# Dividing the softmax of an attention core after its value product, with the reciprocals spread over the rows by an identity product

## The chip, the core and the metric

The kernel is one program on one core of a Trainium2 chip. The metric is device time in microseconds of one execution. The engines named below are PE (TensorE, matmuls), PEld (its weight loads), DVE (VectorE), ACT (ScalarE), POOL (GpSimd) and SP (it issues the DMAs). Each of them takes its instructions strictly in the order in which they stand in its queue, and waits on semaphores for the others.

## The reference

Four layers over 256 context tokens and 256 latent tokens of width 1024. Layers 0 and 3 mix tokens by windowed grouped-query attention with a sink logit for each head, layer 1 by latent attention (MLA), layer 2 by a linear recurrence; a gated MLP with a short convolution follows each. What the change concerns is the softmax and the product behind it:

```python
def attend(q, k, v, mask=None, sink=None):
    s = jnp.einsum("bqhgd,bkhd->bhgqk", q, k, preferred_element_type=jnp.float32) * (q.shape[-1] ** -0.5)
    ...
    m = jnp.max(s, axis=-1)
    ...
    p = jnp.exp(s - m[..., None])
    denom = jnp.sum(p, axis=-1)
    if sink is not None:
        denom = denom + jnp.exp(sk - m)
    o = jnp.einsum("bhgqk,bkhd->bqhgd", p, v.astype(jnp.float32))
    o = o / jnp.transpose(denom, (0, 3, 1, 2))[..., None]
```

## The kernel before

Everything lives feature by token: the stream `X` is eight tiles of 128 features by 512 tokens. Weights come in units of 128 x 1024, one DMA each, and are split into a high and a low part (`whi` by ACT, `wlo` by POOL); a projection is then three matmuls for each tile (lines 231 to 233). Layers 0, 1 and 2 work on all 512 tokens and layer 3 on the latent ones alone.

Attention is cut into *cores*, a function `core` in `swa` (layers 0 and 3) and one in `mla` (layer 1). One core is a block of 128 queries for two heads `z` = 0, 1. There are 32 cores in layer 0 (16 on context blocks with 256 keys, 16 on latent blocks with 512), 32 in layer 1 (16 and 16) and 16 in layer 3 (latent alone): 80 in all. A core does, in this order:

- the scores of both heads into a PSUM bank `mm` (L678, L679; in MLA L920), queries on the partitions;
- the row maximum. In a latent core of `swa` one DVE instruction adds the mask, scales and takes the maximum (L705), and another negates it (L708). Elsewhere it is a reduction and a few small ones;
- the exponentials `P` by ACT with the row sums `den` (L709, L698; in MLA L930), and in `swa` the sink's part of the sum (L711 to L713);
- the reciprocals `rd` of the sums, 128 x 2 (L714, L931);
- the division, on `P`, while the queries are still on the partitions and the reciprocal is a scalar of each partition: in `swa` head 0 by DVE (L719) and head 1 by ACT (L717), in MLA both by DVE (L933);
- the transposes of `P` on PE (L727, L941), copied out of the bank `tp` to `pt` by ACT, in `swa` every second one by DVE (L249, L251);
- the value product into the bank `mo` (L733, L947): head 0 fills partitions 0 to 63 and head 1 partitions 64 to 127, 128 columns (queries) wide;
- `put`, which splits the result into `o` high (ACT, L265) and `o` low (DVE, L266).

Pools set how far cores can overlap: two banks each of `mm`, `tp`, `mo` and `fl`, six tiles `P`, two `pt`. In layer 0 the products that make the modulation vectors (`mod0_steps`, L346) keep one of the two `mo` banks for as long as they last: 26 steps, of which 3 are taken in the projection ahead of the cores and one by each core after, so 23 of the 32 cores share the other bank. Between cores stand projections: those of the next queries or keys in bank `fl`, and the output projection of the first half of the heads.

The order on each engine is set when the program is built, by a scheduler that interleaves the cores with the projections; at run time each engine goes through its list and waits where an input is missing.

Of the kernel before, what the change touches and what calls it, by code (L numbers as in the profile page):

```python
# [14 lines left out]
AF = mybir.ActivationFunctionType  # L15
# [96 lines left out]
def hybrid_kernel(ctx: ExitStack, tc: tile.TileContext, xT, cc, ccT, W, modwa, modwb, modw, colv, rowv, tabs, band, out, depth=DEPTH, dbg=None):  # L112
# [43 lines left out]
    def mo_ps():  # L156
        return ps_mo.tile([128, T], F32, tag="mo", name="mo")
# [84 lines left out]
    def sel(arrs, *idx):  # L242
        return tuple(a[idx] for a in arrs)
# [20 lines left out]
    def split(hi, lo, src):  # L264
        nc.scalar.activation(hi, src, AF.Copy)  # L265
        nc.vector.tensor_tensor(lo, src, f32(hi), op=ALU.subtract)  # L266

    def rsqrt(v, n, steps=3):
        i = small(n, "rs_i", I32)
# [289 lines left out]
    def swa(l, i, q0, nm, nxt, first=None):  # L559
# [87 lines left out]
        def q_post(p, b, ps):  # L647
            if rqs[p] is None:
                rqs[p] = const.tile([128, 32], F32, tag=f"rqs{p}", name="rqs")
            if (p, b // 2) not in qt:  # L650
                qt[p, b // 2] = big("q").rearrange("p (b j) n -> p b j n", b=2)
            qb = qt[p, b // 2][:, b % 2]
            sq = tmp("sq")
            nc.scalar.activation(sq, ps, AF.Square)
            ss = small(8, "ssq")
            nc.vector.tensor_reduce(ss, sq.rearrange("p (h d) -> p h d", d=64), axis=AX.X, op=ALU.add)
            qr = tmp("qr")
            rotate(qr, ps, b, 8, gq, cgq, sgq)
            for z in range(2):
                hl = tmp("qhl")  # L660
                h4 = hl.rearrange("p (h s d) -> p h s d", h=4, s=2)
                q4 = qr[:, z * 256:(z + 1) * 256].rearrange("p (h d) -> p h d", h=4)
                nc.scalar.activation(h4[:, :, 0].bitcast(F32R), q4, AF.Copy)
                nc.vector.tensor_tensor(h4[:, :, 1], q4, h4[:, :, 0], op=ALU.subtract)
                pq = tp_ps()
                for j in range(4):
                    nc.tensor.transpose(pq[:, j * 128:(j + 1) * 128], hl[:, j * 128:(j + 1) * 128], ident)
                if z == 0:
                    nc.scalar.activation(qb[:, z], pq, AF.Copy)
                else:  # L670
                    nc.vector.tensor_copy(qb[:, z], pq)
            rq = mean_rsqrt(ss, 8, 64)
            nc.vector.tensor_scalar(rqs[p][:, b * 8:(b + 1) * 8], rq, 0.125, None, op0=ALU.mult)

        def scores(ps, p, b, j, g, nk):
            h = 2 * j + g
# [4 lines left out]
        def core(p, b, j):  # L681
# [19 lines left out]
            else:  # L701
                for z in range(2):
                    ps, pt = mm_ps(), probs()
                    scores(ps, p, b, j, z, nk)
                    nc.vector.tensor_tensor_reduce(  # L705
                        out=pt, in0=ps, in1=mask[:, b - 2], op0=ALU.add, op1=ALU.max,
                        scale=rq2[:, z:z + 1], scalar=sk[:, z:z + 1], accum_out=mx[:, z:z + 1])
                    nc.vector.tensor_scalar(ngm[:, z:z + 1], mx[:, z:z + 1], -1.0, None, op0=ALU.mult)  # L708
                    nc.scalar.activation(pt, pt, AF.Exp, bias=ngm[:, z:z + 1], accum_out=den[:, z:z + 1])  # L709
                    P.append(pt)  # L710
            nc.vector.tensor_tensor(es, sk, ngm, op=ALU.add)  # L711
            nc.scalar.activation(es, es, AF.Exp)
            nc.vector.tensor_tensor(den, den, es, op=ALU.add)  # L713
            nc.vector.reciprocal(rd, den)  # L714
            for z in range(2):
                if z:
                    nc.scalar.activation(P[z], P[z], AF.Copy, scale=rd[:, z:z + 1])  # L717
                else:
                    nc.vector.tensor_scalar(P[z], P[z], rd[:, z:z + 1], None, op0=ALU.mult)  # L719
            po = mo_ps()[:, :128]  # L720
            pt = pt_p.tile([128, 2, T], F32, tag="pt", name="pt")
            for kp in range(nk // 256):
                pp = tp_ps()
# [5 lines left out]
                for kk in range(2):  # L729
                    kb = 2 * kp + kk  # L730
                    for z in range(2):
                        r = slice(64 * z, 64 * z + 64)
                        nc.tensor.matmul(po[r], v[0][:, kb, p * 128 + 64 * z:p * 128 + 64 * z + 64],  # L733
                                         pt[:, kp, (kk * 2 + z) * 128:(kk * 2 + z + 1) * 128], start=kb == 0, stop=kb == nk // 128 - 1)
            put(sel(o[p], slice(None), j, slice(b * 128, (b + 1) * 128)), po)

        ps = {b: mm_ps() if z < 2 else fl_ps() for z, b in enumerate(range(q0, 4))}
        proj(1, ps, hook=lambda q, done: steps(mods, MQ[q]))
# [27 lines left out]
    def mla(l, nm, nxt):  # L766
# [138 lines left out]
        def core(hg, hp, b):  # L905
# [23 lines left out]
            for z in range(2):  # L929
                nc.scalar.activation(P[z], S[z], AF.Exp, bias=ngm[:, z:z + 1], scale=rq2[:, z:z + 1], accum_out=den[:, z:z + 1])  # L930
            nc.vector.reciprocal(rd, den)  # L931
            for z in range(2):
                nc.vector.tensor_scalar(P[z], P[z], rd[:, z:z + 1], None, op0=ALU.mult)  # L933
            po = mo_ps()[:, :128]
            pt = pt_p.tile([128, 2, T], F32, tag="pt", name="pt")
            for kp in range(nk // 256):
                pp = tp_ps()
# [5 lines left out]
                for kk in range(2):  # L943
                    kb = 2 * kp + kk
                    for z in range(2):
                        c = hp * 128 + 64 * z
                        nc.tensor.matmul(po[64 * z:64 * z + 64], d["v"][:, kb, c:c + 64], pt[:, kp, (kk * 2 + z) * 128:(kk * 2 + z + 1) * 128],  # L947
                                         start=kb == 0, stop=kb == nk // 128 - 1)
            put(sel(o[hg // 2], slice(None), (2 * hg + hp) % 4, bc), po)

        group(0)
        ss = small(16, "ssk")
# [416 lines left out]
```

## Time and profile before

| | us |
|---|---|
| median of 3 runs | 2230.91 (2227.56 to 2233.28) |
| the profiled execution | 2228.39 |
| its span, first to last instruction | 2226.6 |
| PE busy | 2113.2 (95%) |
| PEld busy | 1760.3 (79%) |
| DVE busy | 1563.7 (70%) |
| ACT busy | 1032.2 (46%) |
| POOL busy | 1044.8 (47%) |
| mean granted clock of PE | 0.987 |

The profiled execution took 1.8 us more than its span. The shares are means over stages that differ: in the MLPs PE is busy all the time, in the attention stages (the cores run from 100 to 264 us, 720 to 895 us and 1930 to 2012 us) it waits now and then, and DVE and ACT are fuller. PE counts as busy until a matmul has drained, so that overlapping matmuls make it look fuller than it is; the time of one row is no price of one matmul in a stream of them.

### The profile page before, as it was taken

How to read it: one execution, taken by the hardware profiler on the slowest of the kernel's cores; microseconds unless marked ns; L12 is line 12 of the kernel's file. 1: busy time of each engine (PE TensorE's matmuls, PEld its weight loads, DVE VectorE, ACT ScalarE, POOL GpSimd, SP SyncE). 2: the span in 40 equal slices, each digit the busy share in tenths (PEclk: the TensorE clock that was granted, in tenths of full speed). 3: DMA queues.
4: the chain of work that ended last, by engine and by line, in shares of the span. 5: the costliest groups of instructions: out<-in, count | busy, mean ns of one | idle time of the engine just before them, and what ended most of it. 6: DMA issues, size and time to landing. Idle time of an engine off the chain costs nothing.

```text
span 2226.6 us, 32884 instructions
## 1 busy us (share of the span) xinstructions
PE 2113.2 (95%) x12084; PEld 1760.3 (79%) x12084; DVE 1563.7 (70%) x3342; ACT 1032.2 (46%) x1850; POOL 1044.8 (47%) x760
## 2 busy tenths in 40 slices
PE   6989999999999999999999998899999999898999
PEld 4666788888888666878888886688888888678999
DVE  4677779777786887687888689847864457785333
ACT  4466653222346775532233367534333224675544
POOL 3331255544544113445455446764544444526887
PEclk9999999999999999999999999999999999999999
DMA  7534136554532011255555422234655552313665
GB/s 299 199 123 133 39 123 189 171 177 157 179 116 68 21 29 57 60 189 178 175 184 182 149 67 67 89 94 136 194 183 167 168 161 85 104 39 107 188 182 160
DMA packets 83888, 300.14 MB, mean 135 GB/s; under 512 B 11152, under 2 KB 12816, under 8 KB 81296
## 3 DMA queue, kind: packets, MB, share of 16 engines
q1 hardware_dynamic: 83728, 298.05, 42.2%
q8 instruction: 95, 1.56, 0.3%
q14 instruction: 65, 0.53, 0.1%
HBM read 296.97 MB, written 1.05 MB: 134 GB/s over the span
## 4 chain that ended last, share of the span: by engine, by line
PE 78%; DVE 12%; ACT 3%; DMA 3%; issue 2%; POOL 2%; SPq 0%; ACTq 0%; DVEq 0%; POOLq 0%
PE fl L232 9%; PE fl L233 9%; PE fl L231 9%; PE mm L233 7%; PE mm L232 7%; PE mm L231 7%; PE mo L231 4%; PE mo L232 4%; PE mo L233 4%; PE tp L231 3%; PE tp L232 3%; PE tp L233 3%; PE mo L733 2%; POOL wlo L222 2%; PE mm L920 2%
## 5 line engine op out<-in xcount | busy, mean ns | idle before, releaser
L222 POOL TENSOR_TENSOR wlo<-raw,whi 128x256 fp32r<-128x256 f32 (+3 forms) x709 | 1010.1, 1446 | 1113.3 <-ACT whi L218 1075.1
L218 ACT ACTIVATE whi<-raw 128x1024 fp32r<-128x1024 f32 (+3 forms) x367 | 382.5, 1043 | 489.1 <-PE mm L232 170.4
L380 DVE SCALAR_TENSOR_TENSOR junk<-mw,cbc 128x1024 bf16<-128x1024 f32 x256 | 457.3, 1786 | 26.4 <-DMA mw<-in_modw_dram 15.8
L233 PE MATMUL fl<-h_hi,wlo 128*128 128x512 f32 (+1 forms) x816 | 293.4, 360 | 4.9 <-POOL wlo L222 4.9
L231 PE MATMUL fl<-h_hi,whi 128*128 128x512 f32 (+1 forms) x816 | 293.2, 359 | 1.5 <-DVE xc L1039 1.3
L232 PE MATMUL fl<-h_lo,whi 128*128 128x512 f32 (+1 forms) x816 | 293.2, 359 | 0.0
L232 PE MATMUL mm<-h_lo,whi 128*128 128x512 f32 (+1 forms) x784 | 274.1, 351 | 2.5 <-DVE h_lo L448 1.5
L231 PE MATMUL mm<-h_hi,whi 128*128 128x512 f32 (+1 forms) x784 | 273.9, 351 | 1.2 <-ACT h_hi L442 1.1
L233 PE MATMUL mm<-h_hi,wlo 128*128 128x512 f32 (+1 forms) x784 | 273.5, 349 | 0.0
L1145 DVE SCALAR_TENSOR_TENSOR conv<-mm,colt,conv 128x510 f32<-128x510 f32 (+1 forms) x88 | 59.8, 679 | 190.1 <-ACT conv L1143 190.0
L1149 ACT ACTIVATE conv<-conv 128x512 f32<-128x512 f32 (+1 forms) x88 | 51.0, 579 | 289.3 <-DVE conv L1147 289.3
L233 PEld LDWEIGHTS fl<-h_hi,wlo 128*128 128x128 f32 x816 | 155.0, 190 | 28.6 <-POOL wlo L222 6.1
L231 PEld LDWEIGHTS fl<-h_hi,whi 128*128 128x128 f32 x816 | 155.3, 190 | 24.3 <-ACT P L1058 1.7
L232 PEld LDWEIGHTS fl<-h_lo,whi 128*128 128x128 f32 x816 | 155.0, 190 | 22.1
L232 PEld LDWEIGHTS mm<-h_lo,whi 128*128 128x128 f32 x784 | 149.4, 191 | 23.5 <-POOL h_lo L446 2.5
L231 PEld LDWEIGHTS mm<-h_hi,whi 128*128 128x128 f32 x784 | 149.4, 191 | 20.8 <-ACT h_hi L442 2.1
L233 PEld LDWEIGHTS mm<-h_hi,wlo 128*128 128x128 f32 x784 | 149.5, 191 | 18.6
L454 DVE SCALAR_TENSOR_TENSOR x<-mo,modc,x 128x256 f32<-128x256 f32 x197 | 88.3, 476 | 87.4 <-PE mo L233 87.1
L231 PE MATMUL mo<-g_hi,whi 128*128 128x512 f32 (+1 forms) x388 | 134.3, 346 | 0.6 <-DVE x L454 0.6
L232 PE MATMUL mo<-g_lo,whi 128*128 128x512 f32 (+1 forms) x388 | 134.4, 346 | 0.0
L233 PE MATMUL mo<-g_hi,wlo 128*128 128x512 f32 (+1 forms) x388 | 134.3, 346 | 0.0
L231 PE MATMUL tp<-g_hi,whi 128*128 128x512 f32 (+1 forms) x352 | 124.0, 352 | 1.5 <-DVE x L454 1.5
(331 smaller groups left out, 4427.9 us busy)
## 6 DMA issues: line engine op xcount, KB each, us to landing
raw<-in_W_dram SPq DMA_DIRECT2D x352, 512.0 KB, 3.6
mw<-in_modw_dram SPq DMA_DIRECT2D x144, 512.0 KB, 4.2
mw<-in_modwa_dram SPq DMA_DIRECT2D x8, 1024.0 KB, 14.8
mw<-in_modwb_dram SPq DMA_DIRECT2D x16, 512.0 KB, 4.9
mw<-in_modwb_dram SPq DMA_DIRECT2D x8, 1024.0 KB, 9.1
cbc<-in_cc_dram SPq DMA_DIRECT2D x3, 1024.0 KB, 6.1
raw<-in_W_dram SPq DMA_DIRECT2D x8, 384.0 KB, 3.0
x<-in_xT_dram SPq DMA_DIRECT2D x8, 256.0 KB, 4.7
```

Of the source, the lines that this page charges most:

```text
L218: nc.scalar.activation(hi, raw, AF.Copy)
L222: nc.gpsimd.tensor_tensor(lo[:, cs], raw[:, cs], f32(hi[:, cs]), op=ALU.subtract)
L231: nc.tensor.matmul(ps, ah, bh, start=start and i == 0, stop=False, **kw)
L232: nc.tensor.matmul(ps, ah, bl, start=False, stop=False, **kw)
L233: op = nc.tensor.matmul(ps, al, bh, start=False, stop=stop and i == n - 1, **kw)
L380: nc.vector.scalar_tensor_tensor(junk, raw, 1.0, cbc[:, s], op0=ALU.mult, op1=ALU.mult, accum_out=modc[l][:, s, m:m + 1])
L454: nc.vector.scalar_tensor_tensor(X[m][:, half], ps[:, half], modc[l][:, s, part + m:part + m + 1], X[m][:, half], op0=ALU.mult, op1=ALU.add)
L733: nc.tensor.matmul(po[r], v[0][:, kb, p * 128 + 64 * z:p * 128 + 64 * z + 64], pt[:, kp, (kk * 2 + z) * 128:(kk * 2 + z + 1) * 128], start ...
L920: nc.tensor.matmul(ps[:, c], d["q"][:96, 2 * hp + z, bc], d["k"][:96, 2 * hp + z, :nk], start=True, stop=True)
L1145: op = nc.vector.scalar_tensor_tensor(y3[:, :, 1:], g3[:, :, :255], cw[:, l, 0, f:f + 1], y3[:, :, 1:], op0=ALU.mult, op1=ALU.add)
L1149: nc.scalar.activation(y[:, t0:], y[:, t0:], AF.Silu)
```

## The change

The division moves from `P` to the value product. A new function `divide` gets the whole `mo` bank: columns 0 to 127 hold the value product as before, columns 128 to 255 a second product, made for each head from the reciprocals, broadcast along 64 columns as the stationary operand, and the identity as the moving one. It puts the reciprocal of query n into column n of all 64 rows of a head. ACT copies these 128 x 128 numbers to SBUF (into `P[0]`, which the transposes no longer need), DVE multiplies the value product by them in place, and `put` follows as before. Both scalings of `P` go. In the latent cores of `swa` the scores are taken with the opposite sign (the scale is -0.125 and the maximum becomes a minimum against the negated sink), so that the instruction that negated the maximum (L708) goes too; the exponential turns the sign back by its scale.

```diff
+    def divide(po, rd, room, dst):
+        rb = po[:, 128:256]
+        for z in range(2):
+            nc.tensor.matmul(rb[64 * z:64 * z + 64], rd[:, z:z + 1].to_broadcast([128, 64]), ident, start=True, stop=True)
+        nc.scalar.activation(room, rb, AF.Copy)
+        nc.vector.tensor_tensor(po[:, :128], po[:, :128], room, op=ALU.mult)
+        put(dst, po[:, :128])
...
-            nc.vector.tensor_scalar(rqs[p][:, b * 8:(b + 1) * 8], rq, 0.125, None, op0=ALU.mult)
+            nc.vector.tensor_scalar(rqs[p][:, b * 8:(b + 1) * 8], rq, 0.125 if b < 2 else -0.125, None, op0=ALU.mult)
...
-                        out=pt, in0=ps, in1=mask[:, b - 2], op0=ALU.add, op1=ALU.max,
-                        scale=rq2[:, z:z + 1], scalar=sk[:, z:z + 1], accum_out=mx[:, z:z + 1])
-                    nc.vector.tensor_scalar(ngm[:, z:z + 1], mx[:, z:z + 1], -1.0, None, op0=ALU.mult)
-                    nc.scalar.activation(pt, pt, AF.Exp, bias=ngm[:, z:z + 1], accum_out=den[:, z:z + 1])
+                        out=pt, in0=ps, in1=mask[:, b - 2], op0=ALU.add, op1=ALU.min,
+                        scale=rq2[:, z:z + 1], scalar=nsk2[:, z:z + 1], accum_out=ngm[:, z:z + 1])
+                    nc.scalar.activation(pt, pt, AF.Exp, bias=ngm[:, z:z + 1], scale=-1.0, accum_out=den[:, z:z + 1])
...
-            for z in range(2):
-                if z:
-                    nc.scalar.activation(P[z], P[z], AF.Copy, scale=rd[:, z:z + 1])
-                else:
-                    nc.vector.tensor_scalar(P[z], P[z], rd[:, z:z + 1], None, op0=ALU.mult)
-            po = mo_ps()[:, :128]
+            po = mo_ps()
...
-            put(sel(o[p], slice(None), j, slice(b * 128, (b + 1) * 128)), po)
+            divide(po, rd, P[0][:, :128], sel(o[p], slice(None), j, slice(b * 128, (b + 1) * 128)))
```

In `mla` the core is changed in the same way: its two scalings (L933) go, and `divide` takes the place of `put`. The change moves nothing on any engine outside the three attention stages.

On PE, among the first cores of MLA, the rows stood like this (`mo` is the value product's bank with its number, `tp` that of the transposes, `mm` that of the scores, `fl` a projection's; the row says out<-moving, stationary):

```order
L947 MATMUL mo_6929<-pt_6930,v_6618 64x128 x8
L920 MATMUL mm_6985<-k_6617,q_6616 128x512
L941 MATMUL tp_6967<-tabt_104,P_6955 128x128 x4
L920 MATMUL mm_7081<-k_6617,q_6616 128x256 x2
L947 MATMUL mo_6965<-pt_6966,v_6618 64x128 x4
```

With the change they stand like this at the same place (the scores are L922 now, and L271 is the product with the identity in `divide`):

```order
L947 MATMUL mo_6961<-pt_6962,v_6650 64x128 x8
L271 MATMUL mo_6961<-tabt_104,st_6947 64x128 x2
L941 MATMUL tp_7001<-tabt_104,P_6991 128x128 x4
L922 MATMUL mm_7023<-k_6649,q_6648 128x512
L941 MATMUL tp_7033<-tabt_104,P_7019 128x128
L922 MATMUL mm_7121<-k_6649,q_6648 128x256
L947 MATMUL mo_6999<-pt_7000,v_6650 64x128 x4
L271 MATMUL mo_6999<-tabt_104,st_6989 64x128 x2
```

In every one of the 80 cores the two new matmuls stand directly behind the last value product of their bank.

On DVE, in the same cores, the two scalings of `P` (L933) stood right behind the reciprocal, ahead of the next core's reductions:

```order
L931 RECIPROCAL st_6913<-st_6913 128x2
L266 TENSOR_TENSOR o1_6886<-mo_6899,o0_6885 128x128
L933 TENSOR_SCALAR P_6915<-P_6915,st_6913 128x512
L933 TENSOR_SCALAR P_6920<-P_6920,st_6913 128x512
L928 TENSOR_TENSOR st_6953<-st_6953,rqs_6619 128x2
L924 TENSOR_REDUCE st_6979<-mm_6980 128x1
```

Now the multiplication (L273) stands among the work of later cores and projections, with `o` low (L266) three rows behind it:

```order
L281 TENSOR_SCALAR rs_y_7097<-rs_i_7096 128x8
L273 TENSOR_TENSOR mo_6961<-mo_6961,P_6949 128x128
L283 TENSOR_TENSOR rs_t_7098<-rs_y_7097 128x8
L926 TENSOR_REDUCE st_7017<-mm_7023 128x1
L266 TENSOR_TENSOR o1_6918<-mo_6961,o0_6917 128x128
L927 TENSOR_TENSOR st_7017<-st_7017,rqs_6651 128x1
```

L273 waits for ACT's copy and L266 for ACT's `o` high, so DVE has two places in a core where it waits for ACT behind the value product; before it had one.

## Rows read from the trace of the kernel before

**Rows 1.** Windows view, six stretches of the attention stages and one of an MLP.

```profile
core 0: us, PE busy (x) PEld busy (x) DVE busy (x) ACT busy (x) POOL busy (x), PEclk, DMA share, GB/s
112.00:152.00 40.00, 34.76 (x224) 24.37 (x224) 31.97 (x114) 28.69 (x77) 17.11 (x24) 0.96 0.31 101
152.00:264.00 112.00, 105.95 (x821) 73.95 (x820) 82.83 (x305) 75.30 (x199) 17.67 (x24) 1.00 0.32 105
720.00:850.00 130.00, 118.20 (x785) 85.44 (x786) 106.79 (x390) 92.83 (x228) 20.46 (x31) 0.99 0.10 30
850.00:895.00 45.00, 44.89 (x270) 31.50 (x269) 28.77 (x85) 24.98 (x58) 9.36 (x14) 1.00 0.16 47
1930.00:1980.00 50.00, 44.10 (x328) 31.98 (x326) 46.81 (x178) 37.51 (x92) 8.46 (x12) 0.97 0.11 35
1980.00:2012.00 32.00, 31.54 (x283) 26.82 (x282) 23.88 (x79) 22.51 (x54) 11.63 (x16) 1.00 0.22 67
...
1000.00:1250.00 250.00, 250.00 (x1105) 207.05 (x1104) 198.51 (x276) 75.45 (x93) 126.74 (x47) 1.00 0.56 173
```

**Rows 2.** Waits view of PE: who waited for whom, us, times, longest.

```profile
PE tp L727 <- DVE P L719: 9.6, 8, 2.7
```

**Rows 3.** Timeline of two stretches: start, us, engine, line; idle before it and its releaser.

```profile
120.74 0.30 PE L727 MATMUL tp<-tabt,P 128*128 128x128 f32 x1 [2.23 <-DVE P L719]
...
1950.72 0.72 ACT L709 ACTIVATE P<-P,st 128x512 f32<-128x512 f32 x1 [0.62 <-DVE st L708]
...
1953.43 0.48 DVE L719 TENSOR_SCALAR P<-P,st 128x512 f32<-128x512 f32 x1
...
1954.06 1.22 PE L727 MATMUL tp<-tabt,P 128*128 128x128 f32 x7 [2.67 <-DVE P L719]
```

**Rows 4.** Windows view of two short stretches behind those waits, columns as in group 1.

```profile
121.00:126.00 5.00, 5.00 (x32) 3.56 (x30) 1.78 (x5) 3.77 (x10) 2.16 (x4) 0.66 0.26 98
...
1954.00:1959.00 5.00, 4.94 (x33) 3.68 (x34) 3.58 (x12) 2.56 (x6) 0.00 (x0) 0.66 0.17 70
```

**Rows 5.** Timeline of PE, ACT and DVE around one value product of layer 0.

```profile
160.75 1.09 PE L733 MATMUL mo<-pt,v 128*64 128x128 f32 x16
...
161.78 1.09 PE L727 MATMUL tp<-tabt,P 128*128 128x128 f32 x8
161.90 0.28 ACT L265 ACTIVATE o<-mo 128x128 fp32r<-128x128 f32 x1 [0.68 <-PE mo L733]
162.21 0.29 DVE L266 TENSOR_TENSOR o<-mo,o 128x128 fp32r<-128x128 f32 x1 [1.29 <-ACT o L265]
...
163.12 0.66 PE L733 MATMUL mo<-pt,v 128*64 128x128 f32 x8
```

**Rows 6.** Windows view of L719 alone: DVE busy (instructions).

```profile
112.00:152.00 40.00, 2.65 (x6) 0.96 0.31 101
1930.00:1980.00 50.00, 4.33 (x9) 0.97 0.11 35
```

**Rows 7.** Windows view of L933 alone.

```profile
720.00:850.00 130.00, 18.38 (x48) 0.99 0.10 30
```

**Rows 8.** Windows view of L708 alone.

```profile
112.00:152.00 40.00, 0.57 (x4) 0.96 0.31 101
1930.00:1980.00 50.00, 2.84 (x21) 0.97 0.11 35
```

**Rows 9.** Windows view of L266 alone (one in each core).

```profile
112.00:152.00 40.00, 2.00 (x7) 0.96 0.31 101
720.00:850.00 130.00, 6.92 (x24) 0.99 0.10 30
1930.00:1980.00 50.00, 2.32 (x8) 0.97 0.11 35
```

**Rows 10.** Groups by line and form on DVE: count, busy us, mean ns, idle before.

```profile
L1150 DVE TENSOR_TENSOR fl<-conv,fl 128x256 f32<-128x256 f32 x22 | 9.4, 429 | 13.0 <-ACT conv L1149 13.0
```

**Rows 11.** Line view of L266: what ended DVE's idle time ahead of it, us, times.

```profile
  ACT o L265: 27.1, 33
```

More of the change, by code (lines that the diff above doesn't have):

```diff
@@ L732, in core @@
                         r = slice(64 * z, 64 * z + 64)
-                        nc.tensor.matmul(po[r], v[0][:, kb, p * 128 + 64 * z:p * 128 + 64 * z + 64],
+                        nc.tensor.matmul(po[r, :128], v[0][:, kb, p * 128 + 64 * z:p * 128 + 64 * z + 64],
                                          pt[:, kp, (kk * 2 + z) * 128:(kk * 2 + z + 1) * 128], start=kb == 0, stop=kb == nk // 128 - 1)
-            put(sel(o[p], slice(None), j, slice(b * 128, (b + 1) * 128)), po)
+            divide(po, rd, P[0][:, :128], sel(o[p], slice(None), j, slice(b * 128, (b + 1) * 128)))
         ps = {b: mm_ps() if z < 2 else fl_ps() for z, b in enumerate(range(q0, 4))}
@@ L931, in core @@
             nc.vector.reciprocal(rd, den)
-            for z in range(2):
-                nc.vector.tensor_scalar(P[z], P[z], rd[:, z:z + 1], None, op0=ALU.mult)
-            po = mo_ps()[:, :128]
+            po = mo_ps()
             pt = pt_p.tile([128, 2, T], F32, tag="pt", name="pt")
@@ L946, in core @@
                         c = hp * 128 + 64 * z
-                        nc.tensor.matmul(po[64 * z:64 * z + 64], d["v"][:, kb, c:c + 64], pt[:, kp, (kk * 2 + z) * 128:(kk * 2 + z + 1) * 128],
+                        nc.tensor.matmul(po[64 * z:64 * z + 64, :128], d["v"][:, kb, c:c + 64], pt[:, kp, (kk * 2 + z) * 128:(kk * 2 + z + 1) * 128],
                                          start=kb == 0, stop=kb == nk // 128 - 1)
-            put(sel(o[hg // 2], slice(None), (2 * hg + hp) % 4, bc), po)
+            divide(po, rd, P[0][:, :128], sel(o[hg // 2], slice(None), (2 * hg + hp) % 4, bc))
         group(0)
```

## The prediction

> **What bounds the kernel now.** The page of the profile first: PE is busy 95% of the span, so the question is where it is not full. The windows view tells that. In an MLP stretch, the last row of the group, PE is busy all the time [rows 1]: nothing that the change touches stands there, and the order of the instructions changes in the attention stages alone. Those stages fall into two kinds of stretches. In three of them, 40, 130 and 50 us long, DVE is the engine with the least room: it is busy 31.97 + 106.79 + 46.81 = 185.6 of 220 us [rows 1], in layer 3 even 46.81 of 50, and PE waits. In the rest, 112 + 45 + 32 = 189 us, PE is busy 105.95 + 44.89 + 31.54 = 182.4 us [rows 1]: there PE sets the pace, as far as its busy time can say so.
>
> The waits view then says whether PE waits for the division itself: the transposes waited 9.6 us in 8 waits for DVE's scaling of P [rows 2]. The timeline of the longest shows what such a wait is made of: the exponential of the core's second head began at 1950.72 and took 0.72 us, but the transposes began at 1954.06, because the sink's sum, the reciprocal and the scaling stood in DVE's queue behind other work, and the scaling (1953.43, 0.48 us) came two microseconds after the exponential [rows 3]. The clock pays too: directly behind this wait of 2.67 us, and behind one of 2.23 us at 120.74 [rows 3], the granted clock of the next 5 us is 0.66 on average [rows 4], that is, 1.2 GHz for some two thirds of the time; ahead of them it was 2.4 GHz.
>
> **The change, part by part.**
>
> *Two products more on PE in each of 80 cores.* No row shows a product with a broadcast operand, but the value products have the same shape, 64 columns of weights and 128 moving columns, and also alternate between the two halves of the array. A matmul of this kind gives two records. Sixteen records took 1.09 us and eight took 0.66 us [rows 5], so eight more cost 0.43 us, and the four records of a core's two products 0.215 us. They stand directly behind the value products and their input has long been there, so PE doesn't wait for them. That is the lower bound, 17.2 us for 80 cores. The upper one comes from matmuls that fill the array's whole width, the transposes, with 1.09 us for eight [rows 5], 0.136 us each: if the two halves did not run beside each other, four records would take up to 0.54 us. I take 0.215, from the row that it is nearest to.
>
> *Work taken from DVE.* In the three DVE stretches the scalings take 2.65 + 4.33 us [rows 6] and 18.38 us [rows 7], and the negations 0.57 + 2.84 us [rows 8]: 28.8 us together.
>
> *Work given to DVE.* One multiplication of 128 x 128 out of PSUM and back into PSUM for each core. The nearest row is the subtraction for `o` low, same size, also out of PSUM: 39 of them in these stretches take 2.00 + 6.92 + 2.32 = 11.2 us [rows 9], 0.29 us each. A multiplication that also writes PSUM, twice as wide, takes 0.429 us [rows 10], an upper bound (16.7 us for 39). I take 11.2. The net relief of DVE in these stretches is 28.8 - 11.2 = 17.5 us, at the least 12.1.
>
> *ACT* loses its scaling in `swa` and gains a copy out of PSUM in all cores, 0.28 us by the row of `o` high [rows 5]. It has the more room of the two everywhere in [rows 1] and stays out of the sum.
>
> *The path to the transposes* no longer holds the division; they wait for the exponential alone. The minimum in place of the maximum and the sign in the exponential's scale cost nothing: the instructions stay the same in number and size.
>
> *The path behind the value product* becomes longer. Now it is one round trip: ACT starts 0.05 us after the product's end (160.75 + 1.09), DVE right behind ACT, and the bank is free at 162.50, 0.65 us after the product [rows 5]. With the change it is product, copy, multiplication, `o` high, `o` low: 0.215 + 2 x 0.65 = 1.5 us at best, 0.87 us more. Who waits for it is the next value product in that bank. In layers 1 and 3 two banks cover that. In layer 0 the modulation holds one of them during 23 cores; the next product in [rows 5] began at 163.12, 0.62 us after the bank was free, so it would come 0.25 us late. Half of 23 cores with such a delay make 3 us; bounds are nothing and 23 x 0.87 = 20 us. The outputs `o` are read much later, or, for the last core of a stage, behind the output projections of the first half, which cover 1 us.
>
> **The sum.** In the DVE stretches I count 0.6 of DVE's relief: DVE is busy 84% of that time, and between nothing (the waits are chains between engines and not DVE's load) and all of it this is the nearer side. That is -10.5 us; PE's 39 x 0.215 = 8.4 us go into PE's waits there, which is what the other 0.4 allows for. This holds the transposes' waits, all but about 2 us of them that lie in the other stretches: -2. The two spells of half clock cost 0.34 x 5 = 1.7 us of full-speed work each [rows 4], and go with the waits ahead of them: -3.4. In the PE stretches the products of the other 41 cores cost 41 x 0.215 = +8.8 us. The shared bank in layer 0: +3. Together -10.5 - 2 - 3.4 + 8.8 + 3 = -4.1 us on the profiled execution's 2228.4, so 2224.3. The median of the runs lies 2.5 us above that execution; a median with the change is then 2226.8, say **2227 us**.
>
> PE's busy time may overstate how full the PE stretches are. The Trainium skill says in "Trainium Kernel Development and Optimization", Best Practices, that one should go by the share of weight loading and not by matmul busy time. By that share the PE stretches are 73.95 + 31.50 + 26.82 = 132.3 of 189 us, 70%, against 83% in the MLP (207.05 of 250) [rows 1], so some 15% of the added products could go into gaps, and the sum would be 1.3 us lower. The sum above leaves this out.
>
> **The rivals.** *A gain that shows*: the DVE stretches follow DVE in full (-17.5), and half of the added products in the PE stretches find gaps (+4.4 in place of +8.8), the shared bank costs nothing: -17.5 - 2 - 3.4 + 4.4 = -18.5, that is 2212. For it speaks DVE's 46.81 of 50 us in layer 3; against it, that DVE also idles 34 of the 220 us there, so that chains between engines count too.
>
> *Slower: the second round trip blocks the in-order queues.* DVE waits 27.1 us in all, 33 times, for ACT's `o` high ahead of `o` low [rows 11], with the queue standing still behind it. The change gives it a second such place in each core. If that costs the same again, 39 of 80 cores, 13.2 us, fall on the DVE stretches: -4.1 + 13.2 = +9.1, 2240. It decides from 10.5 us of new idle time ahead of the multiplication there, 0.27 us a core, since DVE's counted relief is then gone. For it: the four steps alternate between two engines. Against it: other work stands between L273 and L266 in DVE's list, and much of that idle time is time in which DVE had nothing else to do.
>
> *Slower: the two halves don't run beside each other.* Then the products cost up to 41 x 0.54 = 22.1 us in the PE stretches in place of 8.8: +9.2, 2240. Against it, the value products with the same pattern do.
>
> **Chances and range.** The forecast (a few microseconds, 2221 to 2233) 0.48, the clear gain 0.22, the round trip 0.20, the halves 0.10. A measurement of this kernel tells 0.3%, 6.7 us, from no change, so "the same" is 2224 to 2238. Of the forecast 0.15 lie below that, 0.31 in it and 0.02 above; of the gain all 0.22 below; of the round trip 0.06 in it and 0.14 above, of the halves 0.05 and 0.05. That makes faster 0.37, same 0.42, slower 0.21. The range leaves out the outer halves of the rivals: 2212 to 2241.
>
> **What would show it.** Right: the transposes wait for ACT's exponential and no longer for DVE; four records of L271 in about 0.22 us; DVE about 17 us less busy in the three stretches, and those shorter by some 10 us; the stretches in which PE is full longer by some 9; no half clock behind the two waits. Wrong: DVE's idle time ahead of L273 of over 10 us, value products that wait for their bank in layer 0, or L271 at 0.4 us and more. The forecast also falls if the new interleaving inside the stages brings waits that none of these rows show; the durations above say nothing about that.

## The result, and the profile after

The changed kernel takes 2242.36 us (median of 5 runs, 2240.37 to 2247.01) beside 2229.6 us for the kernel before on the same chip: a ratio of 1.0054, 95% interval 1.0041 to 1.0067. It is slower by 12 us, where the prediction had it 4 us faster. The profiled execution took 2240.37 us, 12.0 more than the one shown of before.

The first part of the page (busy time, share, instructions) shows PE with 320 matmul records more and DVE lighter by 22.6 us, as the change says:

```profile
PE 2138.4 (96%) x12404; PEld 1778.8 (79%) x12404; DVE 1541.1 (69%) x3246; ACT 1021.6 (46%) x1882; POOL 1040.3 (46%) x760
```

The windows view, over the stretches of [rows 1] moved to where they lie now, and then three short ones for the clock (two behind the places of [rows 4], one new):

```profile
112.00:152.00 40.00, 37.80 (x273) 24.13 (x271) 32.78 (x110) 27.67 (x77) 16.51 (x24) 1.00 0.33 106
724.00:854.00 130.00, 121.68 (x863) 87.60 (x864) 91.44 (x350) 93.32 (x248) 14.64 (x23) 0.97 0.07 22
1943.00:1993.00 50.00, 47.56 (x385) 35.04 (x385) 45.06 (x158) 35.35 (x94) 8.47 (x12) 1.00 0.11 33
...
121.00:126.00 5.00, 4.99 (x42) 3.37 (x40) 4.93 (x14) 3.23 (x11) 3.06 (x4) 1.00 0.74 239
1968.00:1973.00 5.00, 4.69 (x41) 3.54 (x42) 4.93 (x18) 3.11 (x11) 0.00 (x0) 1.00 0.00 0
...
807.00:814.00 7.00, 4.98 (x15) 3.73 (x16) 5.05 (x18) 1.47 (x3) 2.02 (x5) 0.55 0.46 148
```

DVE is busy 32.78 + 91.44 + 45.06 = 169.3 us there, 16.3 less than before. Both spells of half clock that the prediction named are gone. In the middle of MLA there is a new one, at 807. The waits view of PE for the MLA stage says what stands ahead of it (us, times, longest): the transposes of the normed keys, L872, as L870 did in the kernel before.

```profile
PE tp L872 <- DVE rqs L904: 7.8, 2, 4.2
PE tp L872 <- DVE st L933: 2.2, 2, 1.6
...
PE tp L872 <- DVE kn L868: 0.4, 1, 0.4
```

The timeline of one place in layer 0 shows the new steps in order:

```profile
160.18 0.66 PE L735 MATMUL mo<-pt,v 128*64 128x128 f32 x8
...
160.77 0.50 PE L231 MATMUL fl<-whi,h_hi 128*128 128x512 f32 x1
...
161.20 0.66 PE L735 MATMUL mo<-pt,v 128*64 128x128 f32 x8
...
161.69 0.39 PE L271 MATMUL mo<-tabt,st 128*64 128x128 f32 x4
...
162.01 0.50 PE L232 MATMUL fl<-wlo,h_hi 128*128 128x512 f32 x1
...
162.18 0.28 ACT L272 ACTIVATE P<-mo 128x128 f32<-128x128 f32 x1 [2.06 <-PE mo L271]
...
162.49 0.30 DVE L273 TENSOR_TENSOR mo<-mo,P 128x128 f32<-128x128 f32 x1 [2.00 <-ACT P L272]
...
162.83 0.28 ACT L265 ACTIVATE o<-mo 128x128 fp32r<-128x128 f32 x1 [0.36 <-DVE mo L273]
...
163.14 0.29 DVE L266 TENSOR_TENSOR o<-mo,o 128x128 fp32r<-128x128 f32 x1 [0.34 <-ACT o L265]
```

Eight records of the value product and the step to the next matmul took 160.77 - 160.18 = 0.59 us; with the four records of L271 behind them 162.01 - 161.20 = 0.81. So the products cost a core 0.22 us of PE, 17.6 us for 80. The other cores agree: from the start of the last record of a value product to the next matmul it is 0.20 us (median) where no products follow, and 0.42 us (median of all 80 cores) where they do. That is the prediction's size for one core; the prediction charged it to 41 cores only.

Where the time went is read by stage: from the first score to the last value product in layers 0 and 3, from the first to the last value product in MLA. These are starts of instructions in the source view; in MLA, for the kernels before and after:

```profile
L947 PE MATMUL mo<-pt,v x384: 272/273/324, 722.4 to 892.5; 128*64 128x128 f32 x192
```

```profile
L947 PE MATMUL mo<-pt,v x384: 272/273/324, 725.6 to 905.2; 128*64 128x128 f32 x192
```

| stage, us | before | changed | changed, second trace | without products | without products, second trace | no division |
|---|---|---|---|---|---|---|
| layer 0 | 168.0 | 170.3 | 166.1 | 162.1 | 161.7 | 159.3 |
| MLA | 170.1 | 179.6 | 181.3 | 172.8 | 175.2 | 172.4 |
| layer 3 | 83.8 | 83.3 | 83.4 | 78.7 | 79.0 | 80.8 |

(The last four columns are of runs told below.) MLA carries nearly all of the loss. Each column is one execution: the two traces of the changed kernel differ by 4.2 us in layer 0 and by 1.7 us in MLA, so a difference of a few microseconds between two columns is uncertain by about as much.

### The profile page after: what moved, and what is told of

It is laid out like the page before. It is cut to its first block, busy times and chain, and to the rows that moved or that the text cites. A ratio compares the mean times of both kernels' runs of the same rounds, so it can differ in the third digit from the quotient of the medians.

```text
span 2238.6 us, 33496 instructions
## 1 busy us (share of the span) xinstructions
PE 2138.4 (96%) x12404; PEld 1778.8 (79%) x12404; DVE 1541.1 (69%) x3246; ACT 1021.6 (46%) x1882; POOL 1040.3 (46%) x760
```

## The experiments

Theory A: PE pays for the added products in full in all 80 cores, and MLA gives nothing back for the lighter DVE. Theory B: the longer detour over ACT and DVE behind the value product costs the time (the prediction's second rival). All ratios are to the kernel before on the same chip.

**Layers 0 and 3 alone.** MLA's core is the old one.

> The changed kernel with MLA's old core (both scalings of P by DVE, no identity products in layer 1). Theory A, that the added products on PE count in full and the MLA stage gave nothing back for them: the 12 us fell mainly on MLA (+9.9 by the trace), so this is 2232.5 us, some 10 below the changed kernel's 2242.4. Theory B, that the second round trip between ACT and DVE costs its price in every core: 48 of 80 cores keep it, 48/80 of 12.8 us stay, 2237. Theory A predicts shorter MLA waits than the changed kernel's 34.9 us (about 32).

2233.31 us, ratio 1.0014 (1.0003 to 1.0026). The MLA stage is back at 170.1 us. So MLA's part of the loss is 1.0054 less 1.0014, some 9 us for 32 cores, and 48 cores cost 3 us together: A, not B, by which the loss would go by the number of cores.

**The turned sign alone.** The diff's lines on the sign, with the old division.

> The kernel before with the turned sign alone (minimum for maximum, the negation L708 gone), the division still on P. If DVE's load sets the length of its stretches, the 3.4 us of negations there come back as time: 2226. If the waits are chains, the negation counts only where it stands ahead of an exponential that PE waits for, 0.08 us twice a core on 32 cores and a part of that: 2228 to 2230, not to be told from before's 2229.6.

2231.47 us, ratio 0.9999 (0.9987 to 1.0011). Removing L708 gives nothing that can be told.

**No products.**

```diff
-        for z in range(2):
-            nc.tensor.matmul(rb[64 * z:64 * z + 64], rd[:, z:z + 1].to_broadcast([128, 64]), ident, start=True, stop=True)
-        nc.scalar.activation(room, rb, AF.Copy)
+        nc.scalar.activation(room, po[:, :128], AF.Copy)
```

> The changed kernel without the two identity products: ACT's copy reads the value product itself in their place, so that the result is multiplied by itself; copy, multiplication and both parts of the output stay where they were. It leaves out the spreading of the reciprocals. Theory A: 320 records of 0.054 us, 17.4 us, go from PE, and 0.8 to 1 of that from the time: 2225 to 2229. Theory B: the steps behind the value product stay but for 0.2 us, so 2238 to 2242.

2220.52 us, ratio 0.9951 (0.9933 to 0.9969), below A's range too: without the two products the same change is 11 us faster than before.

**No division.** `divide` is `put(dst, po[:, :128])` alone.

> The changed kernel without any division: no identity products, no copy, no multiplication; only the split into high and low part as before. It leaves out the division. Theory A: nothing more than the kernel without the products, within 3 us of it, 2223 to 2228; so the whole of what moving the division off P can give is below 7 us against before. Theory B: some 10 us below the kernel without the products, as the second round trip goes: 2228 to 2232 if that one is at 2240. If DVE's load set the pace after all, 0.6 of the 11 us of multiplications in its stretches would come off too, 7 us below the kernel without products.

2220.24 us, ratio 0.9952 (0.9936 to 0.9968), the same as without the products. The copy, the multiplication and the second round trip cost nothing that can be measured, although DVE stood idle ahead of L273 for 33.2 us in the changed kernel (its line view, whole kernel). B falls.

```profile
  ACT P L272: 33.2, 48
```

The run also gives the most that moving the division off `P` brought here: 11 us, and by the table, one execution against one, all of it in layers 0 (8.7) and 3 (3.0).

**MLA without its scalings.** The loop of L933 is taken out of the kernel before.

> The kernel before without the two scalings of P in the MLA cores (L933); it leaves out the division there, and nothing takes its place. 18.4 us of DVE's work go from the MLA stretch. If the length of that stretch follows DVE's load, as the prediction's share of 0.6 has it, 11 us come off: 2220. If PE's waits there end on the chain that makes the normed keys (the waits ahead of L870 stayed at 8.8 us even with no division at all), nothing comes off: within 3 us of before, 2229 to 2235 beside a before of 2232, and the stage from first to last value product stays at 170 to 173 us.

2230.01 us, ratio 0.9999 (0.9988 to 1.0011). The windows view of the stretch of [rows 1] shows DVE lighter by 15.3 us (it was 106.79), and PE no fuller (118.20):

```profile
720.00:850.00 130.00, 118.12 (x777) 82.80 (x775) 91.50 (x346) 93.60 (x232) 18.42 (x28) 0.99 0.09 26
```

The stage took 171.2 us. So 15 us of DVE's load there did not set the length of that stretch.

**POOL quieter in MLA.** The low part of the three weight units of each head group is left out of the kernel before, the high part stands in for it.

```diff
-            ukv[hg] = unit(("mkv", hg))
-            uq[hg] = [unit(("muq", hg, 0)), unit(("muq", hg, 1))]
+            ukv[hg] = high(("mkv", hg))
+            uq[hg] = [high(("muq", hg, 0)), high(("muq", hg, 1))]
```

> The kernel before with the low part of the three weight units of each MLA head group left out (POOL's subtraction L222 goes for them, the high part stands in for the low one; PE's work is the same). Theory: the small DVE steps of the reciprocal root ahead of the normed keys take 0.65 us in place of 0.17 because POOL works at the same time; without POOL the waits ahead of L870 (10.8 us in all) fall by half or more, 4 to 6 us off the time: 2226 to 2228 beside a before of 2232. Rival: these waits are the order of DVE's queue alone, and nothing changes: 2230 to 2234.

2222.90 us, ratio 0.9963 (0.9949 to 0.9977): 8 us less. The MLA stage took 166.1 us in the trace, 4 less than before, though that trace is of the slowest of the run's eight executions (2230.62 us). So leaving out POOL's work does what leaving out DVE's did not. The timeline of the kernel before shows how, at two places. The first (POOL, then DVE and PE):

```profile
793.72 5.03 POOL L222 TENSOR_TENSOR wlo<-raw,whi 128x256 fp32r<-128x256 f32 x7 [35.74 <-ACT whi L218]
```

```profile
793.62 0.17 DVE L275 TENSOR_TENSOR rs_t<-rs_y 128x8 f32<-128x8 f32 x1
793.82 0.64 DVE L276 SCALAR_TENSOR_TENSOR rs_t<-rs_t,rs_v 128x8 f32<-128x8 f32 x1
794.50 0.66 DVE L277 SCALAR_TENSOR_TENSOR rs_y<-rs_t,rs_y 128x8 f32<-128x8 f32 x1
...
797.26 0.91 DVE L865 TENSOR_TENSOR kn<-kraw,rs_y 128x256 f32<-128x256 f32 x1
```

```profile
799.04 0.61 PE L870 MATMUL tp<-tabt,kn 128*96 128x128 f32 x4 [2.05 <-DVE rqs L902]
```

The small steps of the reciprocal root on the way to the normed keys take 0.17 us until POOL's subtractions begin, and 0.65 us as long as they last; PE waits 2.05 us at the end of that chain. The same steps with that burst of POOL left out (the lines of this run's kernel are six higher):

```profile
793.62 0.17 DVE L281 TENSOR_TENSOR rs_t<-rs_y 128x8 f32<-128x8 f32 x1
793.82 0.17 DVE L282 SCALAR_TENSOR_TENSOR rs_t<-rs_t,rs_v 128x8 f32<-128x8 f32 x1
794.02 0.17 DVE L283 SCALAR_TENSOR_TENSOR rs_y<-rs_t,rs_y 128x8 f32<-128x8 f32 x1
794.22 0.42 DVE L871 TENSOR_TENSOR kn<-kraw,rs_y 128x256 f32<-128x256 f32 x1
```

```profile
796.22 0.60 PE L876 MATMUL tp<-tabt,kn 128*96 128x128 f32 x4
```

The wait is gone. The second place has the longest of these waits, and the run did not touch it: that burst of POOL splits weights of the output projection. Before, and in this run:

```profile
838.84 5.72 POOL L222 TENSOR_TENSOR wlo<-raw,whi 128x256 fp32r<-128x256 f32 x8 [36.68 <-ACT whi L218]
```

```profile
844.84 0.66 PE L870 MATMUL tp<-tabt,kn 128*96 128x128 f32 x4 [3.75 <-DVE rqs L902]
```

```profile
841.39 1.06 PE L876 MATMUL tp<-tabt,kn 128*96 128x128 f32 x4 [3.77 <-DVE rqs L908]
```

Where POOL's burst went the wait went, and where it stayed the wait stayed. In the stage PE's waits for the normed keys fall from 10.8 to 6.1 us, and one of 2.31 us ahead of the stage, at 706 us, to 0.42. That is some 6 of the 8 us; the rest was not traced. The Trainium skill states in "SBUF — State Buffer", Who interferes with whom, that a DVE instruction with two SBUF inputs contends with a GpSimd instruction that reads SBUF; the slow ones here are of that kind.

**Each product twice** (`for z in (0, 1, 0, 1)`).

> The changed kernel with the two identity products made twice in each core. If the 23 us that the kernel without them saved are a price of each product (0.144 us for one of 64 x 128), this costs 23 us more than the changed kernel: 2265. If a part of it is a fixed cost of the place (a wait that one pair brings and a second one doesn't), the second pair costs its records alone, 80 x 0.215 = 17 us: 2259. If products of this kind fit into PE's waits after the first, less than 10 us: below 2252.

2253.16 us, ratio 1.0099 (1.0086 to 1.0112): 10 us more than the changed kernel. At its place the second pair costs what the first does; the timeline of PE:

```profile
171.56 0.66 PE L735 MATMUL mo<-pt,v 128*64 128x128 f32 x8
172.05 0.61 PE L271 MATMUL mo<-tabt,st 128*64 128x128 f32 x8
172.58 0.98 PE L729 MATMUL tp<-tabt,P 128*128 128x128 f32 x7
```

From the value product to the next matmul it is 1.02 us: 0.59 without products, 0.81 with one pair, and 0.21 more with two. The stages took 171.7, 186.8 and 85.5 us, together 12 more than the mean of the two traces with one pair, so less than the 17 that 80 places ask for.

**The division in the transposes.** With the turned sign; the identity of the transposes becomes a diagonal matrix of the reciprocals.

```diff
+        nc.vector.tensor_scalar(dg[:, 0], ident, rd[:, 0:1], None, op0=ALU.mult)
+        nc.scalar.activation(dg[:, 1], ident, AF.Copy, scale=rd[:, 1:2])
...
-                        nc.tensor.transpose(pp[:, c:c + 128], P[z][:, (2 * kp + kk) * 128:(2 * kp + kk + 1) * 128], ident)
+                        nc.tensor.matmul(pp[:, c:c + 128], P[z][:, (2 * kp + kk) * 128:(2 * kp + kk + 1) * 128], dg[:, z], start=True, stop=True)
```

> A version meant to beat both: with the turned sign, the division goes into the transposes, whose identity is replaced by a diagonal matrix of the reciprocals (128 x 128 for each head, head 0 by DVE and head 1 by ACT); no product is added and behind the value product there is only the split. Theory A: PE has no added work, DVE loses most of its scaling, the chain to the transposes is only some 0.3 us shorter than before: between the kernel without any division (2220) and before (2231), 2223 to 2228. Rival: the wait of the transposes for the reciprocals returns in full with the half clock behind it, and nothing is won: 2229 to 2233.

2288.79 us, ratio 1.0254 (1.0239 to 1.0269). Neither theory had the reason: an f32 product of this shape has two records where a transpose has one. The source view of the transposes' line in `swa`, of the kernel before and of this one:

```profile
L727 PE MATMUL tp<-tabt,P x320: 270/273/476, 104.5 to 2009.0; 128*128 128x128 f32 x160
```

```profile
L732 PE MATMUL tp<-junk,P x640: 270/275/378, 105.0 to 2064.2; 128*128 128x128 f32 x160
```

With MLA's 192 that is 512 records more; four full-width records take 0.66 us (the row of L870 above) and seven 0.98 (that of L729), so 0.107 each and 55 us together, against 57 measured. That the totals agree so well is in part luck: layer 0, MLA and layer 3 were 14, 29 and 13 us longer than before, where their 192, 192 and 128 records ask for 21, 21 and 14. "Perfetto Trace Analysis" in the Trainium skill, Transposes, asks for a transpose where one is meant and not a matmul; here a matmul in its place has twice the records.

**The reciprocals spread by transposes.** Half the records; each transpose goes to partitions 0 to 63, so that ACT copies twice. First in all cores, then in layers 0 and 3 alone.

```diff
-            nc.tensor.matmul(rb[64 * z:64 * z + 64], rd[:, z:z + 1].to_broadcast([128, 64]), ident, start=True, stop=True)
-        nc.scalar.activation(room, rb, AF.Copy)
+            rb = po[:64, 128 + 128 * z:256 + 128 * z]
+            nc.tensor.transpose(rb, rd[:, z:z + 1].to_broadcast([128, 64]), ident)
+            nc.scalar.activation(room[64 * z:64 * z + 64], rb, AF.Copy)
```

> The changed kernel with the reciprocals spread by transposes in place of products: a transpose gives one record where a product gives two, so a core's four records of 0.054 us become two; both go to partitions 0 to 63, and ACT copies each half to its place (two copies of 64 x 128 in place of one of 128 x 128). If the price is PE's records: half of 17.4 us comes back, 8.7 off the changed kernel, 2233 beside its 2242. If the price is the detour over the two engines behind the value product (longer by one copy now): no gain or a loss, 2242 to 2248. The answer is the reference's.

> The same transposes in the cores of layers 0 and 3 alone; MLA keeps the old core, since without its scalings its stage was no shorter. Meant to beat both kernels: without a division those layers gave 11 us together (measured: no division at all -11 us, none of it from MLA), 48 cores with two records of 0.054 us take 5.2 back: 5 to 6 us below before, 2224 to 2226 beside a before of 2230. Rival: the two copies and the detour cost what the products did, then it is where the kernel with the products in these layers alone was, 3 us above before.

2247.73 us, ratio 1.0082 (1.0063 to 1.0101), and 2238.97 us, 1.0045 (1.0028 to 1.0062): both missed, no gain over the products. All 160 transposes stood apart in PE's list, and each took 0.13 us until the next matmul could start, 0.27 for a core against 0.22 with the products. For 48 cores that is 2 us of the 7 by which the second version is slower than the one with products (1.0014); what the rest is was not found. One of the 160:

```profile
740.55 0.30 PE L271 MATMUL mo<-tabt,st 128*64 128x128 f32 x1
740.68 0.60 PE L896 MATMUL tp<-tabt,qn 128*96 128x128 f32 x4
```

**The changed kernel and the one without products again**, on one chip.

> The changed kernel once more, on the chip of these runs, to set the price of the first pair of products (23 us by two chips) beside that of the second pair (10 us) more closely. If both are the same price, 16 to 17 us each, this ends 1.2 to 1.3 parts in a hundred of the way: a ratio to before near 1.003 and 16 us above the kernel without products of the same chip; if the first pair is dearer, 20 us or more above it.

> The changed kernel without the identity products once more, on the same chip as the changed kernel (it leaves out the spreading, as before). Same price for both pairs: 16 to 17 us below the changed kernel. Dearer first pair: 20 us or more below it.

2242.99 us, ratio 1.0063 (1.0044 to 1.0083), and 2219.96 us, 0.9955 (0.9938 to 0.9973). The first pair costs 23 us again.

**The transposes next to each other**, both ahead of the two copies, in all cores and in layers 0 and 3.

> The transposed spread with a core's two transposes directly behind each other (both ahead of the two copies); the number of records and of copies is that of the kernel in which they stood apart. If the place is what costs (each change between 64 columns and full width), 80 of 160 places go, 0.13 us each: 10 us less than there (2247.7), 2236 to 2239, and by the records alone 8.7 us below the changed kernel, 2234. If the two copies and the detour behind the value product cost it, this stays at 2245 to 2249. The answer is the reference's.

> The same pair of neighbouring transposes in layers 0 and 3 alone, the old core in MLA. By places: 6 us below the kernel in which they stood apart (2239), 2232 to 2234, so about level with before's 2230; by records: 2225. If the copies and the detour cost it: 2237 to 2241.

2254.57 us, ratio 1.0108 (1.009 to 1.0125), and 2234.49 us, 1.0015 (1.0001 to 1.003). In layers 0 and 3 the time fell by the 6 us that the price by places asks for. In all cores it lost: layer 0 fell from 172.7 to 166.6 us, but MLA grew from 180.1 to 192.8. There the waits for the normed keys rose from 7.5 to 14.7 us, and the transposes of `P` now waited 14 times for ACT's exponential (3.9 us); why was not tested. The pair itself is no cheaper than the products:

```profile
170.68 0.66 PE L736 MATMUL mo<-pt,v 128*64 128x128 f32 x8
171.27 0.41 PE L271 MATMUL mo<-tabt,st 128*64 128x128 f32 x2
171.51 0.93 PE L730 MATMUL tp<-tabt,P 128*128 128x128 f32 x7
```

From value product to next matmul 0.83 us, 0.24 more than without. Two transposes apart cost 0.27, so the places gave some 1.4 us in 48 cores and not 6: that this expectation was met is luck, and what gave the rest stays open.

**One transpose of full width**, one copy by ACT; the reciprocal instruction writes 64 copies for each head. In all cores and in layers 0 and 3.

> The changed kernel with the reciprocals written in 64 copies for each head (the reciprocal instruction itself makes them, 128 x 128 in place of 128 x 2) and spread by one transpose of full width and one copy. If TensorE's time at the place is the price, a core pays 0.109 us in place of 0.218: 8.7 us below the changed kernel, 2234 beside its 2242. DVE pays for it with a longer reciprocal; if a load on DVE counts after all, 80 times 0.2 us of it give this back and it stays at 2242 or above. The answer is the reference's.

> The same in layers 0 and 3 alone, the old core in layer 1. 48 times 0.109 us less than the kernel with the products there (2233, 3 us above before): 2228, 2 us below before, which five rounds can hardly tell from it. If the longer reciprocal counts: 2233 to 2238.

2250.32 us, ratio 1.0088 (1.0074 to 1.0102), and 2237.57 us, 1.0034 (1.002 to 1.0048). The expectation mis-sized the reciprocal: 0.95 us, where that of 128 x 2 takes 0.16, so these two don't test the price on PE.

```profile
L275 DVE RECIPROCAL junk<-st x80: 937/946/954, 104.3 to 2024.9; 128x128 f32<-128x128 f32 x80
```

**The same with a plain copy by DVE** (0.23 us) behind a reciprocal of 128 x 2.

> One transpose of full width in each of the 80 cores, its operand made by a copy of VectorE (128 x 128, some 0.2 us) behind a reciprocal of 128 x 2. If TensorE's time at the place is the price: 0.109 us for a core in place of 0.218, 8.7 us below the changed kernel, 2234, a ratio of 1.002. If VectorE's load counts, 80 times 0.2 us take it back: 2245 or more, as where the reciprocal made the copies (1.0088). The answer is the reference's.

> The same in layers 0 and 3 alone, the old core in layer 1: by TensorE's time 48 times 0.109 us below the kernel with products there (1.0014), so 2228, a ratio of 0.999; level with before as far as five rounds tell. If VectorE's load counts in these layers, where taking it away gave 11 us: 2233 or more (1.0015 to 1.0035).

2241.63 us, ratio 1.0051 (1.0034 to 1.0068), and 2230.93 us, 0.9997 (0.9982 to 1.0011). The first lies between the two values expected, the second between 2228 and 2233, so neither decides. At its place a core now pays 0.76 us from value product to next matmul, 0.17 more than without:

```profile
169.78 0.66 PE L744 MATMUL mo<-pt,v 128*64 128x128 f32 x8
170.37 0.33 PE L281 MATMUL mo<-tabt,junk 128*128 128x128 f32 x1
170.54 0.93 PE L738 MATMUL tp<-tabt,P 128*128 128x128 f32 x7
```

That is 0.05 us a core below the products, 4 us for 80 and 2.4 for 48, where 0.109 a core was expected. The changes of 1.0054 and 1.0063 to 1.0051 (1 to 3 us), and of 1.0014 to 0.9997 (4 us), are of that size but within their intervals. The version for layers 0 and 3 is level with the kernel before; none of these beats it.

## Why the prediction was wrong

Two steps failed, and two smaller terms as well.

**The products in the DVE stretches.** The step was "PE's 39 x 0.215 = 8.4 us go into PE's waits there, which is what the other 0.4 allows for". They don't. The price of one core was right (0.22 us), the two halves of the array do run beside each other, but by the first pair it is paid in every core. Between the traces without and with the products (means of two each) layer 0 grew by 6.3 us, MLA by 6.5 and layer 3 by 4.5: 17.2 us, where 80 x 0.215 is 17.2. The prediction counted 8.8. The windows view of the MLA stage, of the kernel before and of two traces each of the changed kernel and of the one without products (columns as in [rows 1]):

```profile
722.40:892.50 170.10, 158.22 (x1033) 113.53 (x1033) 133.03 (x467) 115.25 (x281) 29.82 (x44) 0.99 0.12 35
```

```profile
725.60:905.20 179.60, 167.84 (x1154) 120.80 (x1155) 122.14 (x438) 120.26 (x312) 29.47 (x44) 0.97 0.11 34
```

```profile
721.90:903.10 181.20, 169.28 (x1154) 121.28 (x1155) 122.39 (x438) 120.34 (x312) 29.44 (x44) 0.96 0.11 33
```

```profile
718.50:891.30 172.80, 159.32 (x1032) 113.04 (x1033) 119.21 (x438) 120.71 (x312) 29.73 (x44) 0.98 0.11 35
```

```profile
716.20:891.40 175.20, 161.64 (x1032) 114.46 (x1033) 119.04 (x438) 120.63 (x312) 29.76 (x44) 0.96 0.11 34
```

PE idles 11.9 us of the stage before, 11.8 and 11.9 with the products, and 13.5 and 13.6 without them: at most 1.7 us of the 7 that 32 cores pay went into its waits. For the PE stretches the prediction weighed a rule of the Trainium skill ("Trainium Kernel Development and Optimization", Best Practices: go by the share of weight loading, not by matmul busy time) and read from it that some of the products could go into gaps of PE, without putting that into the sum; the lengths of the stages show none for the first pair. A likely reason, argued and not tested, is that PE's waits are ends of chains in which PE itself is a link, so a matmul put into its list delays the chain as well.

**The share of 0.6 of DVE's relief, in MLA.** Of the 17.5 us, 18.38 - 6.92 = 11.5 lie in the MLA stretch and stood in the sum with 6.9. They gave nothing: with the scalings simply left out the time stayed (0.9999). DVE is busy 82% of that stretch, but PE's waits there are for one chain, the reciprocal root ahead of the normed keys (10.8 of the 11.9 us that PE idles in the stage), and the long ones last as long as POOL's subtractions make them. The rows that would have told this were in the trace of before (the waits of L870, the 0.65 us beside POOL's burst); the prediction looked at DVE's share of busy time, which these stretched instructions even raise.

**The clock.** The term of -3.4 us for the two spells of half clock was not gained on the whole. Both went, but the MLA stage now spends more time at 1.2 GHz: its granted clock is 0.99 before, 0.97 and 0.96 in the two traces after, and 0.98 and 0.96 without the products. Reckoned as the prediction did (length times one less the clock), 1.7 us of work are lost there before, some 5 and 7 after. One of the spells, at 807, comes with a longer wait of the keys, 4.2 us in place of 2.05. The extra loss is about the size of the part of MLA's growth that the products don't explain: without them that stage was still 2.7 and 5.1 us longer than before. Which changes of order bring these spells was not tested.

**The shared bank.** The +3 us in layer 0 was not there: PE's waits view of that stage has no wait of a value product for `o` high or `o` low, and the line view of L735, which takes in the weight loads, has 0.4 us once for each.

Setting the two failed steps right gives -4.1 + 8.4 + 6.9 = +11.2, against 12.0 between the profiled executions. That this is so near is partly luck. By the stages (means of two) the products cost 17.2 us and MLA without them was 3.9 longer, while layers 0 and 3 without them were 6.1 and 5.0 shorter, 11.1, where the sum had 10.5 - 6.9 + 2 + 3.4 - 3 = 6.0: together +10.0.

**What held.** The transposes of `P` no longer wait for DVE's scaling (9.6 us before [rows 2]); the longest that is left of their waits in layer 0 is 1.5 us, for queries. DVE got 16.3 us lighter (17.5 predicted). The relief was real in layers 0 and 3.

**The rivals.** The clear gain needed the relief in MLA. The second round trip, whose 2240 is near the result, is not the reason for it: DVE's new idle time ahead of L273 in the three stretches is below the 10.5 us that it asked for, 3.8 + 3.6 + 1.3 = 8.7 by the line view of each:

```profile
  ACT P L272: 3.8, 3
...
  ACT P L272: 3.6, 10
...
  ACT P L272: 1.3, 2
```

and taking the whole detour away gave nothing (2220.52 and 2220.24 us). The halves did run beside each other.

**What stays open.** By the medians the first pair of products costs 23 us, twice, and the second 10; at their places both cost 17; by the stages the first costs 17 and the second 12. The two pairs together agree better (1.0099 - 0.9953 is 32.6 us, 16.3 a pair; by the stages 29, 14.6 a pair). Part of the difference is the clock: the runs without products, with one pair and with two lose on average 30.7, 33.0 and 28.7 us to the lower clock (an estimate, the span times one less the granted clock of each run). With that taken out the first pair costs 21 us and the second 14. Where the other 7 us of the difference lie was not found. One rival was not tested: taking instructions out or in also changes the order that the scheduler gives the others (several hundred of PE's 12080 other matmul records stand elsewhere without the products). So the runs without products, without division, without MLA's scalings and with each product twice change the order as well as the work; the run with POOL quieter keeps the order on PE, DVE and ACT.

## What to carry to other kernels

A busy engine beside a waiting one does not mean that the waiting one follows it: ask what the longest waits end on, and leave the suspected work out once; if the time stays, the load was not the limit. Work added to PE's list can be paid for even in stretches where PE waits, as here, so a spread of 0.22 us a core must be set against the gain of the same core: the division off `P` was worth 11 us in 48 cores and nothing in 32, and 80 spreads cost 17 us or more. The price of a matmul depends on its neighbours: a record of the products behind others of their width cost 0.05 us, a transpose of 64 columns ahead of full-width matmuls 0.13, and one of full width behind 64-column products 0.17, where full-width records in a stream cost 0.107 each. So count from the matmul before it to the one behind it, not by records. And an agreement of totals proves little: more than one sum above came out near the measurement over terms that did not.

## What the runs showed of the hardware

- DVE instructions of 128 x 8 with two inputs in SBUF took 0.65 us in place of 0.17 while POOL subtracted 128 x 256 tiles, and one of 128 x 256 took 0.91 in place of 0.42.
- The step from 64-column products to the next full-width matmul: eight of them and the step took 0.59 us, while eight more records in a stream cost 0.43 [rows 5]. The Trainium skill says in "TensorEngine Tiling (Array Packing)", Key Properties, that a change of tiling mode drains the engine; the 0.16 us are in line with that, though no run isolates a drain.
- A full-width f32 transpose has one record, an f32 matmul of the same shape two (320 against 640 in `swa`), and the kernel with 512 of them in place of transposes was 57 us slower.
- A reciprocal of 128 x 128 took 0.95 us on DVE, a copy of that size 0.23.
